# The end of a two-block network on one core: last columns in two quarters, square root on ScalarE, two engines and two queues for the output

## The chip, the cores and the metric

The kernel runs on one core of one Trainium2 chip. The metric is the device time of one execution, in microseconds (us). Three timed runs of the kernel before gave 1130.78, 1130.99 and 1131.72 us; their median, 1130.99 us, is the time before.

## The reference

The program computes two network blocks in fp32 on 256 tokens of width 1024: two hybrid layers (mLSTM, gated linear attention and sparse attention side by side), and then a block of a SwiGLU layer, a mixing layer and a second SwiGLU layer. What the change touches is the very end of it, the down projection of the last SwiGLU layer, its residual sum, and the normalization of the result:

```python
h = h + 0.5 * swiglu(rmsnorm_2(h, ffn2_norm[l]), ffn2_w_gate[l], ffn2_w_up[l], ffn2_w_down[l])
return rmsnorm_2(h, final_norm)

def rmsnorm_2(x, g):
    xf = x.astype(jnp.float32)
    y = xf * lax.rsqrt(jnp.mean(xf * xf, axis=-1, keepdims=True) + EPS)
    return (y * g.astype(jnp.float32)).astype(x.dtype)
```

A row of 1024 numbers can only be scaled once the sum of its squares is known, that is after the last column of the projection has been added to it.

## The kernel before

The 256 tokens are two row tiles of 128 (t = 0, 1), and `x`, the residual stream, stays in SBUF as 128 x 2 x 1024. Every product is made of three fp32r matmuls (`mm3`, L156): weights and activations are split into a high and a low part, and hi x hi, hi x lo and lo x hi are summed in PSUM. Weights come in units of 128 x 1024, which ScalarE copies to the high part (L123) and VectorE reduces to the low part (L124).

`out_proj` makes the last projection. Its output, two tiles by two halves of 512 columns, fills four PSUM banks `op{half}{tile}`. All groups of input rows but the last two run for both tiles at once. The last two groups run bank by bank in the order (t, half) = (0,0), (0,1), (1,0), (1,1), each 12 matmuls of 512 columns (`rows`, two groups of two 128-row slices of three matmuls), so that the banks finish one after the other. After each bank comes `residual` (L333): VectorE reads the 512 columns from PSUM and adds half of them to `x`.

After the second bank of a tile, `write` normalizes the tile through `normed`: ScalarE squares both halves into `xs` (as a throw-away) with a sum per row (L318, an ACTIVATE and the read of its accumulator), VectorE adds the two sums and EPS (L320), GpSimd raises the 128 x 1 result to the power -0.5 (L321), and VectorE scales both halves by it and by the gain (L325, `scalar_tensor_tensor`). Each half goes out through a DMA on SyncE's queue (L1118, 256 KB).

Each engine executes its instructions in the order in which they stand in its program. At this place the order is written out by hand: `out_proj` collects the instructions of ScalarE in a list `act` and those of VectorE in a list `dve`, and `order` chains each list. TensorE's order is that of the calls. The tiles `xs` come from a pool `t2` of 7 slots, `ss` and `r` from the pool `const`. In SBUF the pools lie one behind the other: the weights' (`wr`, `ws`), `big` (with `x` and the transposed activations), `const`, a small gap, `t2`, a gap, and the tiles of the stage (`yh`, `hh`, `fg` and so on).

Of the kernel before, what the change touches and what calls it, by code (L numbers as in the profile page):

```python
# [10 lines left out]
AF = mybir.ActivationFunctionType  # L11
ALU = mybir.AluOpType
# [3 lines left out]
P = 128  # L16
# [4 lines left out]
EPS = 1e-6  # L21
# [3 lines left out]
LEAD = 500  # L25
# [9 lines left out]
class Net:  # L35
# [141 lines left out]
            by_token(t, ps[t])  # L177
        self.tick()

    def rows(self, ps, x, k0, first, last, toks, w):  # L180

        for k in range(2):
            ww = [z[:, 512 * k:512 * (k + 1)] for z in w]
            for t in toks:
                xs = [z[:, k0 + k, P * t:P * (t + 1)] for z in x]
                self.mm3(ps[t], ww, xs, True, first and k == 0, last and k == 1)

    def proj_b(self, x, name, n=2):

# [135 lines left out]
            st.append(nc.vector.scalar_tensor_tensor(xs[h], self.x[:, t, sl], r, g[:, sl], ALU.mult, ALU.mult))  # L325
        return xs, (sq, st, pw)

    def residual(self, t, half, ps, scale=None):
        sl = self.x[:, t, 512 * half:512 * (half + 1)]
        if scale is None:  # L330
            return self.nc.vector.tensor_add(sl, ps, sl)
        else:
            return self.nc.vector.scalar_tensor_tensor(sl, ps, scale, sl, ALU.mult, ALU.add)  # L333

    def out_proj(self, y, nk, scale=None, need=0):


        done = self.begin_next()
        ps = [[self.acc([P, 512], f"op{h}{t}") for t in range(2)] for h in range(2)]
        n = nk // 2  # L340
        for g in range(n - 2):
            if g == need:
                self.join()
            for h in range(2):
                self.rows(ps[h], y, 2 * g, g == 0, False, (0, 1), self.weights())
                self.tick()
        if need >= n - 2:
            self.join()
        ws = [[self.weights() for h in range(2)] for g in range(2)]
        more = self.next_gain is not None  # L350
        units = [self.fetch()] if more else []
        act = [units[0][1][0]] if more else []
        dve = [units[0][1][1]] if more else []
        for t in range(2):
            for h in range(2):
                for g in range(2):
                    self.rows(ps[h], y, 2 * (n - 2 + g), False, g == 1, (t,), ws[g][h])
                    if more and (t, h, g) == (1, 1, 0):
                        units += [self.fetch(), self.fetch(self.third)]
                        act += [units[1][1][0], units[2][1][0]]  # L360
                        dve.append(units[1][1][1])
                        if self.third:
                            self.order([last, units[2][1][1]])
                        for a, b in self.turn():
                            act.append(a)
                            dve.append(b)
                        if not self.third:
                            dve.append(units[2][1][1])
                        dve.append(early)
                with self.tc.high_priority(self.ahead(2 * LEAD)):  # L370
                    early = self.residual(t, h, ps[h][t], scale)
                if not more or (t, h) != (1, 0):
                    dve.append(early)
            if more and t == 1:
                units.append(self.fetch())
                act.append(units[3][1][0])
                dve.append(units[3][1][1])
            self.turn = done(t)
            act += self.steps[0]
            dve += self.steps[1]  # L380
            last = self.steps[2]
        self.order(act)
        self.order(dve)
        self.ready = [u[0] for u in units]
# [722 lines left out]
    def begin_next(self):  # L1107

        if self.next_gain is not None:
            self.xn, fill = self.norm(self.next_gain)  # L1110
            return fill
        g = self.row_bc(self.a["final_norm_2"], D, "g_bc")

        def write(t):
            with self.tc.high_priority(self.ahead(2 * LEAD)):
                halves, self.steps = self.normed(t, g)
                for h, xs in enumerate(halves):
                    self.nc.sync.dma_start(self.out[0, P * t:P * (t + 1), 512 * h:512 * (h + 1)], xs)  # L1118
            return lambda: None

        return write
# [10 lines left out]
def layouts(np, ins):  # L1132
# [18 lines left out]
    for l in range(2):  # L1151
        w = g("w_in")[l]
        m = np.zeros((1024, P), f)
        for o, c, n in ((0, C_IK, 64), (64, C_MLF, 4), (68, C_GA, 16), (84, C_IW, 8), (96, C_MLI, 4)):
            m[:, o:o + n] = w[:, c:c + n]
        misc[64:68, l] = g("ml_b_f")[l]
        misc[96:100, l] = g("ml_b_i")[l]
        units += pa(w, C_DQ) + pb(w, C_IQ, 512) + pb(m, 0, P) + pa(w, C_DK) + pb(w, C_GQ, 256) + pb(w, C_GK, 256)
        head = lambda h: pb(w, C_MLQ + 256 * h, 256) + pb(w, C_MLK + 256 * h, 256)
        units += pa(w, C_DV) + pb(w, C_DZ, 512) + pa(w, C_GV) + pa(w, C_MLV) + pa(w, C_MLO) + head(0) + pa(w, C_GR)  # L1160
        units += pa(w, C_MLV + 512) + head(1) + pa(w, C_MLO + 512) + head(2) + pa(w, C_MLZ) + head(3) + pa(w, C_MLZ + 512)
        units += rows(g("w_out")[l], (1536, 1792, 1024, 1280, 0, 256, 512, 768))

    def ffn(n):
        wg, wu, wd = (g(f"ffn{n}_w_{z}_2")[0] for z in ("gate", "up", "down"))
        out = pa(wg, 0) + pa(wu, 0)
        for c in range(512, DFF, 256):
            out += pb(wg, c, 256) + pb(wu, c, 256)
        return out + rows(wd, range(0, DFF, 256))
# [4 lines left out]
    for n in ("attn", "gmlp"):  # L1174
        wb = g(f"w_branch_{n}_2")[0]
        units += [tiles(wb[:, c:c + 256]) for c in range(0, 1024, 256)]
    units += rows(g("w_out_2")[0], range(0, 1024, 256))
    units += ffn(2)

# [71 lines left out]
```

## Time and profile before

| | |
|---|---|
| median of three runs | 1130.99 us |
| the profiled execution | 1133.35 us |
| its span, first to last instruction | 1131.6 us |
| TensorE busy | 1118.4 us, 99% of the span |
| VectorE busy | 810.8 us, 72% |
| ScalarE busy | 616.3 us, 54% |
| mean granted clock of TensorE | 0.996 of full speed |

The profile is one execution of the program; its times are us from the first instruction. The span is shorter than the execution's time by 1.75 us, which lie before its first and after its last instruction. PE is TensorE, PEld its weight loads, DVE VectorE, ACT ScalarE, POOL GpSimd, SP SyncE, which issues DMAs. Matmuls overlap: each takes longer than the distance to the next. A row of the timeline merges equal instructions that follow each other, and names in brackets what ended the idle time before it.

### The profile page before, as it was taken

The page shows a single profiled execution, that of the slowest core. Times are in us where ns is not written, and L with a number is a line of the kernel's source. Part 1 is how long each engine was busy: PE and PEld are TensorE (multiplying, and loading weights), DVE is VectorE, ACT ScalarE, POOL GpSimd, SP SyncE. Part 2 cuts the span into 40 slices and gives each one's busy share as a digit, 9 for nine tenths or more (in the row PEclk, how much of TensorE's full clock was granted, in tenths as well). Part 3 has the DMA queues.
Part 4 walks back from the last instruction along what each step waited for, and adds up shares of the span by engine and source line. Part 5 has one row for each costly group of instructions (what it writes and reads, how often), then busy time and mean ns, then how long its engine had stood idle before and what let it go on. Part 6 is the DMA issues. An engine that isn't in the chain of part 4 may idle for free.

```text
span 1131.6 us, 16690 instructions
## 1 busy us (share of the span) xinstructions
PE 1118.4 (99%) x6330; PEld 962.3 (85%) x6330; DVE 810.8 (72%) x1233; ACT 616.3 (54%) x950; POOL 105.0 (9%) x136
## 2 busy tenths in 40 slices
PE   8999999999999999999999999999999999999997
PEld 5888889898898989899888888887888998888886
DVE  5688897786568879778747777646698676777743
ACT  4645854564465575456535555444566545555532
POOL 1111102121111210112100000000010001000000
PEclk8999999999999999999999999999999999999999
DMA  8846644455574654455557665666754566666662
GB/s 261 269 151 188 191 153 151 157 168 184 161 216 150 186 182 135 133 160 167 177 165 222 188 191 190 195 188 190 226 182 144 174 189 184 195 188 190 197 190 74
DMA packets 59464, 203.74 MB, mean 180 GB/s; under 512 B 6700, under 2 KB 9652, under 8 KB 59384
## 3 DMA queue, kind: packets, MB, share of 16 engines
q1 hardware_dynamic: 59384, 202.68, 58.3%
q8 instruction: 50, 0.82, 0.3%
q14 instruction: 30, 0.25, 0.1%
HBM read 201.46 MB, written 2.11 MB: 180 GB/s over the span
## 4 chain that ended last, share of the span: by engine, by line
PE 95%; DVE 3%; ACT 1%; DMA 1%; issue 0%; SPq 0%; POOL 0%; DVEq 0%; POOLq 0%; ACTq 0%
PE op L156 20%; PE fg L209 6%; PE fu L209 6%; PE mq L156 4%; PE mk L156 4%; PE mo L156 4%; PE mz L156 4%; PE mv L156 4%; PE fg L210 3%; PE fu L210 3%; PE gatep L209 3%; PE dq L156 2%; PE dz L156 2%; PE brp L156 2%; PE iq L156 2%; PE dk L156 2%
## 5 line engine op out<-in xcount | busy, mean ns | idle before, releaser
L124 DVE TENSOR_TENSOR lo<-raw,hi 128x1024 fp32r<-128x1024 f32 x359 | 443.1, 1236 | 217.1 <-ACT hi L123 216.1
L123 ACT CAST hi<-raw 128x1024 fp32r<-128x1024 f32 x362 | 379.0, 1048 | 371.6 <-PE op L156 91.8
L209 PE MATMUL fu<-x,hi 128*128 128x512 f32 x288 | 101.0, 394 | 0.0
L209 PE MATMUL fg<-x,hi 128*128 128x512 f32 x288 | 100.8, 394 | 0.0
L210 PE MATMUL fg<-x,lo 128*128 128x256 f32 x288 | 79.9, 277 | 0.0
L210 PE MATMUL fu<-x,lo 128*128 128x256 f32 x288 | 79.8, 277 | 0.0
L156 PE MATMUL op<-hi,hh 128*128 128x512 f32 x176 | 68.6, 390 | 0.0
L156 PE MATMUL op<-lo,hh 128*128 128x512 f32 x176 | 68.5, 389 | 0.0
L156 PE MATMUL op<-hi,hl 128*128 128x512 f32 x176 | 68.5, 389 | 0.0
L209 PEld LDWEIGHTS fg<-x,hi 128*128 128x128 f32 x288 | 54.0, 188 | 12.6
L209 PEld LDWEIGHTS fu<-x,hi 128*128 128x128 f32 x288 | 54.0, 188 | 12.5
L321 POOL TENSOR_TENSOR r<-r,mhalf 128x1 f32<-128x1 f32 x12 | 6.7, 555 | 528.5 <-DVE r L320 528.5
L210 PEld LDWEIGHTS fg<-x,lo 128*128 128x128 f32 x288 | 54.1, 188 | 0.1
L210 PEld LDWEIGHTS fu<-x,lo 128*128 128x128 f32 x288 | 54.1, 188 | 0.0
L156 PE MATMUL op<-hi,yh 128*128 128x512 f32 x128 | 51.1, 399 | 0.0
L156 PE MATMUL op<-lo,yh 128*128 128x512 f32 x128 | 50.0, 391 | 0.0
L156 PE MATMUL op<-hi,yl 128*128 128x512 f32 x128 | 49.9, 390 | 0.0
L156 PE MATMUL mq<-x,hi 128*128 128x256 f32 x256 | 48.2, 289 | 0.0
L156 PE MATMUL mk<-x,hi 128*128 128x256 f32 x256 | 46.8, 284 | 0.0
L209 PE MATMUL gatep<-x,hi 128*128 128x512 f32 x128 | 46.1, 403 | 0.0
L697 DVE SCALAR_TENSOR_TENSOR cacc<-pad,cols,cacc 128x256 f32<-128x256 f32 x96 | 41.0, 479 | 0.0
L156 PE MATMUL mv<-hi,x 128*128 128x512 f32 x128 | 40.7, 399 | 0.0
(361 smaller groups left out, 2598.7 us busy)
## 6 DMA issues: line engine op xcount, KB each, us to landing
raw<-in_w SPq DMA_DIRECT2D x362, 512.0 KB, 3.6
x<-in_x SPq DMA_DIRECT2D x2, 512.0 KB, 5.1
g_bc<-in_norm_g SPq DMA_DIRECT2D x2, 512.0 KB, 4.5
mlg<-in_ml_norm_g SPq DMA_DIRECT2D x2, 512.0 KB, 5.1
skew<-strips SPq DMA_DIRECT2D x4, 256.0 KB, 5.2
pen<-skew SPq DMA_DIRECT2D x8, 128.0 KB, 2.9
mb<-M SPq DMA_DIRECT2D x2, 512.0 KB, 4.3
g_bc<-in_ffn_norm SPq DMA_DIRECT2D x2, 512.0 KB
```

Source lines behind the costliest of these rows:

```text
L123: a = nc.scalar.copy(hi, raw)
L124: b = (nc.gpsimd if pool else nc.vector).tensor_tensor(lo, raw, hi.bitcast(F32), ALU.subtract)
L156: self.nc.tensor.matmul(out, lhsT=lhsT, rhs=rhs, start=first and i == 0, stop=last and i == 2)
L209: nc.tensor.matmul(ps, lhsT=wh[:, ks], rhs=self.x2[:, k], start=k == 0, stop=False)
L210: nc.tensor.matmul(ps[:, 1, :], lhsT=wl[:, ks], rhs=self.x2[:, k, 0, :], start=False, stop=k == KT - 1)
L321: pw = nc.gpsimd.tensor_tensor(r, r, self.mhalf[:, 0:1], ALU.pow)
L697: nc.vector.scalar_tensor_tensor(acc[:, c, :], pad[:, c, 1 + i:1 + i + S], w(i), acc[:, c, :], ALU.mult, ALU.add)
```

## The change

The last bank, (t, half) = (1,1), is made in two quarters of 256 columns. The first quarter is finished in its old bank; the last two groups of the second quarter go into a bank of their own, `op_late`, so that the old bank can be read while TensorE writes the new one. The first residual still adds all 512 columns of the old bank (the second quarter has the sum of the earlier groups there), and a second one adds the 256 columns of `op_late`.

The normalization of the last stage is a function of its own, `last`, for both tiles. The sum of squares is taken of three parts, 512, 256 and 256 columns. VectorE multiplies the first half of `x` by the gain before the scale is known (`mult`, L339), and adds EPS and the first two sums (`add`, L340). The third sum goes in as the input and that sum as the bias of a square root on ScalarE (L342); VectorE takes the reciprocal (L343). Then ScalarE scales the first half (L344) and issues its DMA on its own queue (L345), while VectorE scales the second half (L346), which SyncE stores (L347). GpSimd's power falls away here. The lists `act` and `dve` get the new instructions in a written order.

```diff
--- before.py
+++ after.py
@@ -177,13 +177,13 @@
             by_token(t, ps[t])
         self.tick()
 
-    def rows(self, ps, x, k0, first, last, toks, w):
+    def rows(self, ps, x, k0, first, last, toks, w, cols=slice(0, 512)):
 
         for k in range(2):
-            ww = [z[:, 512 * k:512 * (k + 1)] for z in w]
+            ww = [z[:, 512 * k + cols.start:512 * k + cols.stop] for z in w]
             for t in toks:
                 xs = [z[:, k0 + k, P * t:P * (t + 1)] for z in x]
-                self.mm3(ps[t], ww, xs, True, first and k == 0, last and k == 1)
+                self.mm3(ps[t][:, cols], ww, xs, True, first and k == 0, last and k == 1)
 
     def proj_b(self, x, name, n=2):
 
@@ -325,8 +325,32 @@
             st.append(nc.vector.scalar_tensor_tensor(xs[h], self.x[:, t, sl], r, g[:, sl], ALU.mult, ALU.mult))
         return xs, (sq, st, pw)
 
-    def residual(self, t, half, ps, scale=None):
-        sl = self.x[:, t, 512 * half:512 * (half + 1)]
+    def last(self, t, g, out):
+
+
+
+        nc = self.nc
+        x = self.x[:, t, :]
+        ss = self.small([P, 4], "ss4")
+        xs = [self.tmp([P, 512], f"xs{h}") for h in range(2)]
+        hs = [slice(512 * h, 512 * (h + 1)) for h in range(2)]
+        parts = [(0, hs[0]), (1, slice(512, 768)), (1, slice(768, 1024))]
+        sq = [nc.scalar.activation(xs[h][:, c.start - 512 * h:c.stop - 512 * h], x[:, c], AF.Square, scale=1.0 / 32, accum_out=ss[:, i:i + 1]) for i, (h, c) in enumerate(parts)]
+        mult = nc.vector.tensor_tensor(xs[0], x[:, hs[0]], g[:, hs[0]], ALU.mult)
+        add = nc.vector.scalar_tensor_tensor(ss[:, 3:4], ss[:, 0:1], EPS, ss[:, 1:2], ALU.add, ALU.add)
+        r = self.small([P, 2], "r2")
+        root = nc.scalar.activation(r[:, 0:1], ss[:, 2:3], AF.Sqrt, bias=ss[:, 3:4])
+        rec = nc.vector.reciprocal(r[:, 1:2], r[:, 0:1])
+        m = nc.scalar.mul(xs[0], xs[0], r[:, 1:2])
+        nc.scalar.dma_start(out[:, hs[0]], xs[0])
+        st = nc.vector.scalar_tensor_tensor(xs[1], x[:, hs[1]], r[:, 1:2], g[:, hs[1]], ALU.mult, ALU.mult)
+        nc.sync.dma_start(out[:, hs[1]], xs[1])
+        self.marks = mult, add
+        return sq + [root, m], [rec, st], None
+
+    def residual(self, t, half, ps, scale=None, cols=slice(0, 512)):
+        sl = self.x[:, t, 512 * half + cols.start:512 * half + cols.stop]
+        ps = ps[:, cols]
         if scale is None:
             return self.nc.vector.tensor_add(sl, ps, sl)
         else:
@@ -353,6 +377,14 @@
         dve = [units[0][1][1]] if more else []
         for t in range(2):
             for h in range(2):
+                if not more and (t, h) == (1, 1):
+                    late = [None, self.bank([P, 512], "op_late")]
+                    for z, cols in ((ps[h], slice(0, 256)), (late, slice(256, 512))):
+                        for g in range(2):
+                            self.rows(z, y, 2 * (n - 2 + g), z is late and g == 0, g == 1, (t,), ws[g][h], cols)
+                        with self.tc.high_priority(self.ahead(2 * LEAD)):
+                            dve.append(self.residual(t, h, z[t], scale, cols if z is late else slice(0, 512)))
+                    break
                 for g in range(2):
                     self.rows(ps[h], y, 2 * (n - 2 + g), False, g == 1, (t,), ws[g][h])
                     if more and (t, h, g) == (1, 1, 0):
@@ -376,6 +408,10 @@
                 act.append(units[3][1][0])
                 dve.append(units[3][1][1])
             self.turn = done(t)
+            if not more:
+                mult, add = self.marks
+                dve.insert(len(dve) - 2 * t, mult)
+                dve.append(add)
             act += self.steps[0]
             dve += self.steps[1]
             last = self.steps[2]
@@ -1113,9 +1149,7 @@
 
         def write(t):
             with self.tc.high_priority(self.ahead(2 * LEAD)):
-                halves, self.steps = self.normed(t, g)
-                for h, xs in enumerate(halves):
-                    self.nc.sync.dma_start(self.out[0, P * t:P * (t + 1), 512 * h:512 * (h + 1)], xs)
+                self.steps = self.last(t, g, self.out[0, P * t:P * (t + 1)])
             return lambda: None
 
         return write
```

ScalarE's program at its end before; `xs_10683` and `xs_10684` are the halves of tile 0, `xs_10721` and `xs_10722` those of tile 1:

```order
L123 CAST hi<-raw 128x1024 x16
L318 ACTIVATE xs_10683,ss<-x 128x512
L318 ACTIVATE xs_10684,ss<-x 128x512
L318 ACTIVATE xs_10721,ss<-x 128x512
L318 ACTIVATE xs_10722,ss<-x 128x512
```

ScalarE's program at the same place now; tile 1 has `xs_10738` and `xs_10739`:

```order
L123 CAST hi<-raw 128x1024 x16
L338 ACTIVATE xs_10683,ss_10682<-x 128x512
L338 ACTIVATE xs_10684,ss_10682<-x 128x256 x2
L342 ACT_TABLE_LOAD
L342 ACTIVATE r_10690<-ss_10682 128x1
L344 ACTIVATE xs_10683<-xs_10683,r_10690 128x512
L345 DMA out<-xs_10683 128x512
L338 ACTIVATE xs_10738,ss_10737<-x 128x512
L338 ACTIVATE xs_10739,ss_10737<-x 128x256 x2
L342 ACTIVATE r_10745<-ss_10737 128x1
L344 ACTIVATE xs_10738<-xs_10738,r_10745 128x512
L345 DMA out<-xs_10738 128x512
```

Between the squares of tile 0 and those of tile 1 ScalarE now has a table load, the root, a scaling and a DMA; the load stands once, ahead of the first root.

VectorE's program at its end before:

```order
L333 SCALAR_TENSOR_TENSOR x<-op_10304,x 128x512
L333 SCALAR_TENSOR_TENSOR x<-op_10306,x 128x512
L320 SCALAR_TENSOR_TENSOR r<-ss 128x1
L325 SCALAR_TENSOR_TENSOR xs_10683<-x,r,g_bc 128x512
L325 SCALAR_TENSOR_TENSOR xs_10684<-x,r,g_bc 128x512
L333 SCALAR_TENSOR_TENSOR x<-op_10305,x 128x512
L333 SCALAR_TENSOR_TENSOR x<-op_10307,x 128x512
L320 SCALAR_TENSOR_TENSOR r<-ss 128x1
L325 SCALAR_TENSOR_TENSOR xs_10721<-x,r,g_bc 128x512
L325 SCALAR_TENSOR_TENSOR xs_10722<-x,r,g_bc 128x512
```

VectorE's program at the same place now, with the semaphores of engines that each instruction waits for:

```order
L357 SCALAR_TENSOR_TENSOR x<-op_10306,x 128x512 [waits PE_49]
L339 TENSOR_TENSOR xs_10683<-x,g_bc 128x512 [waits Activation_49]
L340 SCALAR_TENSOR_TENSOR ss_10682<-ss_10682 128x1 [waits Activation_49]
L343 RECIPROCAL r_10690<-r_10690 128x1 [waits Activation_49]
L346 SCALAR_TENSOR_TENSOR xs_10684<-x,r_10690,g_bc 128x512 [waits DVE_49]
L357 SCALAR_TENSOR_TENSOR x<-op_10305,x 128x512 [waits PE_49]
L339 TENSOR_TENSOR xs_10738<-x,g_bc 128x512 [waits Activation_49]
L357 SCALAR_TENSOR_TENSOR x<-op_10307,x 128x512 [waits PE_49]
L357 SCALAR_TENSOR_TENSOR x<-op_late,x 128x256 [waits DVE_49,PE_49]
L340 SCALAR_TENSOR_TENSOR ss_10737<-ss_10737 128x1 [waits Activation_49]
L343 RECIPROCAL r_10745<-r_10745 128x1 [waits Activation_49]
L346 SCALAR_TENSOR_TENSOR xs_10739<-x,r_10745,g_bc 128x512 [waits DVE_49]
```

The residual of bank (1,0), `x<-op_10305`, still stands behind tile 0's normalization, now behind its reciprocal and one scaling; the product `xs_10738<-x,g_bc` of tile 1 waits for ScalarE and stands ahead of the residual of the last bank.

On TensorE the last 12 matmuls of 512 columns are now 24 of 256; ahead of them nothing differs in the programs of the engines. In SBUF the new `ss4` and `r2` have two buffers each of 32 bytes (the smallest piece) behind the other tiles of `const`, so the tiles of `t2` and of the stages lie 128 bytes higher (the first slot of `t2` at 111488 in place of 111360).

## Rows read from the trace of the kernel before

**Rows 1.** The page, part 1: each engine's busy time, share, instructions.
```profile
PE 1118.4 (99%) x6330; PEld 962.3 (85%) x6330; DVE 810.8 (72%) x1233; ACT 616.3 (54%) x950; POOL 105.0 (9%) x136
```
**Rows 2.** Timeline, TensorE: start, duration, the last matmuls of banks (1,0) and (1,1).
```profile
1121.40 0.39 PE L156 MATMUL op<-lo,hh 128*128 128x512 f32 x1
...
1124.12 0.39 PE L156 MATMUL op<-lo,hh 128*128 128x512 f32 x1
```
**Rows 3.** Timeline of VectorE from bank (0,1) on.
```profile
1119.10 0.69 DVE L333 SCALAR_TENSOR_TENSOR x<-op,x 128x512 f32<-128x512 f32 x1 [2.03 <-PE op L156]
1120.59 0.16 DVE L320 SCALAR_TENSOR_TENSOR r<-ss 128x1 f32<-128x1 f32 x1 [0.79 <-ACT xs L318]
1121.48 1.41 DVE L325 SCALAR_TENSOR_TENSOR xs<-x,r,g_bc 128x512 f32<-128x512 f32 x2 [0.73 <-POOL r L321]
1122.82 0.68 DVE L333 SCALAR_TENSOR_TENSOR x<-op,x 128x512 f32<-128x512 f32 x1
1124.54 0.69 DVE L333 SCALAR_TENSOR_TENSOR x<-op,x 128x512 f32<-128x512 f32 x1 [1.05 <-PE op L156]
1126.02 0.16 DVE L320 SCALAR_TENSOR_TENSOR r<-ss 128x1 f32<-128x1 f32 x1 [0.79 <-ACT xs L318]
1126.91 1.42 DVE L325 SCALAR_TENSOR_TENSOR xs<-x,r,g_bc 128x512 f32<-128x512 f32 x2 [0.73 <-POOL r L321]
```
**Rows 4.** Timeline of ScalarE: squares of banks (0,1) and (1,1).
```profile
1119.83 0.63 ACT L318 ACTIVATE xs<-x 128x512 f32<-128x512 f32 x1 [2.00 <-DVE x L333]
...
1125.27 0.63 ACT L318 ACTIVATE xs<-x 128x512 f32<-128x512 f32 x1 [1.01 <-DVE x L333]
1125.80 0.19 ACT L318 ACTIVATION_READ_ACCUMULATOR xs<-x 128x1 f32 x1
```
**Rows 5.** Timeline of GpSimd: the power of tile 1.
```profile
1126.33 0.55 POOL L321 TENSOR_TENSOR r<-r,mhalf 128x1 f32<-128x1 f32 x1 [4.88 <-DVE r L320]
```
**Rows 6.** Timeline of SyncE's queue: the last two stores' issues.
```profile
1127.69 0.33 SPq L1118 DMA_DIRECT2D out<-xs  x1
1128.35 0.33 SPq L1118 DMA_DIRECT2D out<-xs  x1
```
**Rows 7.** SyncE's waits from 1115 on: total us, times, longest.
```profile
SPq L1247 <- DMA out<-xs: 1.7, 1, 1.7
```
**Rows 8.** Windows: length, busy (count) by engine, clock, DMA share, GB/s.
```profile
1127.69:1128.52 0.83, 0.00 (x0) 0.00 (x0) 0.64 (x1) 0.00 (x0) 0.00 (x0) 1.00 0.00 0
1128.52:1130.04 1.52, 0.00 (x0) 0.00 (x0) 0.00 (x0) 0.00 (x0) 0.00 (x0) 0.63 0.91 345
```
**Rows 9.** Chain of waits: start, length, piece; 256-column matmuls.
```profile
895.03 23.03 PE brp L156 x192
```
**Rows 10.** Timeline of ScalarE around a table load.
```profile
115.84 1.04 ACT L123 CAST hi<-raw 128x1024 fp32r<-128x1024 f32 x1
116.90 1.28 ACT L640 ACT_TABLE_LOAD   x1
118.19 0.64 ACT L640 ACTIVATE ltmp<-ltmp 128x512 f32<-128x512 f32 x1
```
**Rows 11.** Groups on ScalarE: shapes, count | busy us, mean ns | idle.
```profile
L738 ACT ACTIVATE mjunk<-hp 128x256 f32<-128x256 f32 x16 | 6.5, 407 | 7.4 <-DVE hp L727 7.2
L628 ACT ACTIVATE lg<-lg,smax 128x256 f32<-128x256 f32 x16 | 8.0, 499 | 1.3 <-DVE smax L626 1.3
L519 ACT ACTIVATE iw<-iwT 128x8 f32<-128x8 f32 x4 | 0.5, 168 | 0.0
```
**Rows 12.** Groups on VectorE, the same columns.
```profile
L908 DVE TENSOR_TENSOR fs<-fs,fu 128x512 f32<-128x512 f32 x22 | 15.0, 690 | 0.6
L217 DVE SCALAR_TENSOR_TENSOR qk<-qk2p,qk 128x256 f32<-128x256 f32 x4 | 1.7, 417 | 0.0
```
**Rows 13.** Timeline of VectorE: small instructions that depend on each other.
```profile
550.59 0.16 DVE L724 SCALAR_TENSOR_TENSOR rd<-nd,rd 128x1 f32<-128x1 f32 x1
550.78 0.16 DVE L725 RECIPROCAL rd<-rd 128x1 f32<-128x1 f32 x1
```

## The prediction

> **What bounds the kernel now.** I read the page first: TensorE is busy for 99% of the span [rows 1], so a change behind its last matmul can touch only the last few microseconds. Then the timelines of the engines from 1115 on, as one chain. TensorE starts its last matmul at 1124.12 [rows 2]. VectorE adds the last bank from 1124.54, ScalarE squares it from 1125.27 and has read its sum at 1125.99 [rows 3, 4], VectorE adds the sums at 1126.02, GpSimd's power runs from 1126.33 for 0.55 [rows 5], and VectorE scales both halves from 1126.91 to 1128.33. SyncE issues the two stores at 1127.69 and 1128.35 [rows 6].
>
> What ends last is not the second scaling. From 0.83 after the first issue the 16 DMA engines are 91% busy for 1.52 us, until 1130.04 [rows 8]: the second store's data queue up behind the first's. So the end is set by the first store's issue, plus 0.83, plus 1.52 for 512 KB. SyncE's wait for them is over at 1128.35 + 0.33 + 1.73 = 1130.41 [rows 6, 7], and the barrier behind it ends the span at 1131.6.
>
> The second thing to see is a queue on VectorE: bank (1,0) is complete at about 1121.82 (its last matmul starts 2.72 before that of (1,1), whose residual starts 0.42 after it), but its residual starts at 1122.82 [rows 2, 3], since it stands behind the scalings of tile 0. Before, this lateness dies out: the next residual waits for TensorE again.
>
> **The change, step by step, on the clock of that execution.** Four rules from the rows: an engine starts 0.03 after another's end that released it (1125.23 to 1125.27 in rows 3 and 4); a dependent VectorE instruction 0.03 after the one before it [rows 13]; an independent one about 0.08 before its end (two L325 of 0.75 in 1.41) [rows 3]; the sum of a 512-column square is ready 0.72 after its start [rows 4].
>
> TensorE: 24 matmuls of 256 columns in place of 12 of 512. 192 of 256 took 23.03 [rows 9], so 0.12 each, 2.88 in all against 2.72 for 12: +0.16. A short one is finished a little sooner; `op_late` is complete at about 1124.7 and the old bank at about 1123.25.
>
> Tile 0. The residual of (0,1) ends at 1119.79. Two 256-column squares follow; one takes 0.41 [rows 11], and with their sums they end at about 1120.73. VectorE's product (0.69 [rows 12]) and small sum lie beside them. Then the new thing: Sqrt needs another table, and its load takes 1.28 [rows 10], until 1122.03. The root itself has no row. From below it is the 128x8 ACTIVATE of 0.17, from above the 128x256 one with a bias per row, 0.50 [rows 11]; I take 0.26, the small one plus what such an operand adds (0.499 - 0.407), being nearest to it. Root until 1122.30, reciprocal (0.16 [rows 13]) until 1122.49, scaling of the second half on VectorE from 1122.53 to 1123.28. So bank (1,0)'s residual starts at 1123.20, 0.4 later than now. ScalarE scales its half until about 1123.25 and then issues a DMA; if that holds it as long as SyncE's issue, 0.33 [rows 6], it is free at 1123.6, before it is needed.
>
> Tile 1. Residual (1,0) until 1123.88, its square from 1123.92, its sum at 1124.64. Here is the added wait: the product of `x` and the gain writes the buffer into which the square was thrown away, so VectorE waits for ScalarE, until 1124.67, and then takes 0.69. Behind it stand the residuals of the last bank, of which the first had been ready since 1123.25. It runs from 1125.28 to 1125.97, the second (0.42, the 256-column row [rows 12]) depends on it and runs until 1126.42. TensorE's quarters are ready 2 and 1.3 us before VectorE takes them, so splitting the bank hides nothing as long as VectorE is behind.
>
> The last square starts at 1126.45 and has its sum after 0.49 at 1126.95 (0.41, and 0.08 until its sum is read); the first quarter's square lies before it, the small sum beside it. Root until 1127.24, reciprocal until 1127.43, ScalarE's scaling (0.63 [rows 4] plus 0.09 for the operand per row) until 1128.18 and VectorE's (0.75) until 1128.21. Both stores are issued at about 1128.21 to 1128.24, against 1127.69 and 1128.35 now.
>
> **The two queues.** The pair of stores is bound by 512 KB at 345 GB/s [rows 8] and not by its issues, so issuing them together takes nothing off the 1.52; if anything the earlier first issue of now was worth more. The end moves as the first issue does: 1128.21 - 1127.69 = **+0.52 us**.
>
> The Trainium skill, "DMA: Bandwidth & Descriptors", section "Issuing engines are not separate DMA queues", speaks against this part of the change: DMAs from several issuing engines run on the same 16 DMA engines and only issue time is saved. The trace agrees, with 91% busy. Were the queues separate, the pair would take half of 1.52 and the sum be -0.2.
>
> **Where the time was saved and given back.** From the last residual to the first store the chain gets shorter: now 1124.54 to 1127.69, 3.15; then, from the second quarter's residual at 1126.00 to 1128.21, 2.21. The small residual and square give 0.27 and 0.22, and the sum and the power with their hand-overs (1125.99 to 1126.91, 0.92) become root and reciprocal with theirs (1126.95 to 1127.46, 0.51). That is the 0.9 gained; but the chain starts 1.46 later, at 1126.00 in place of 1124.54. Nearly all of these 1.46 are the table load and the product in front of the residuals.
>
> **Bounds.** With roots of 0.17, +0.34; with roots of 0.50, +1.0. If the scaling costs ScalarE no more than a square, -0.1. If the first DMA on ScalarE's queue needs longer to its data than 0.83, the SyncE store covers it in part. So +0.2 to +1.1. The profiled execution's own time was 1133.35, that is 1131.6 of span and 1.75 around it; it becomes 1133.9 with a span of 1132.1. The median of the runs stands 2.36 lower, and I add the same 0.52: 1131.5.
>
> **Rivals.**
> *The load isn't paid.* If the table is in place before tile 0's squares end, or the load runs beside them, tile 0 is 1.31 earlier, VectorE meets bank (1,0) as it completes, the product is out of the way by 1124.1, and the second quarter is taken at 1124.7: -0.8 us, 1130.2. For it: ScalarE is idle for 2.00 just before the second square of tile 0 [rows 4], room enough for a load. Against: the load stands in its program behind the squares, and it starts only when its turn comes. 12%.
>
> *A switch of tables costs more than the load.* On the path of tile 0 every addition counts in full. In the trace the copy ahead of the load ends at 116.88, the load takes 116.90 to 118.18, and the next one starts at 118.19 [rows 10]: 1.31 in all; against it, then. An addition as large as the load itself would give +0.52 + 1.28, about +1.8: 1132.8. 6%.
> The Trainium skill, "ScalarE: Activation LUTs", section "What ACT_TABLE_LOAD costs", counts 1283 ns and a drain of about 1380 ns, 2.66 us for a switch; by it the sum would be +1.9. The row has the 1283 and no room for the drain.
>
> *The moved tiles cost something.* All tiles behind `const` lie 128 bytes higher, and so does what TensorE reads of them for 1118 us. If each of its 6330 matmuls took 0.4 ns longer, the kernel would be 2.5 us slower, 1133.5; from 0.36 ns on it decides against no change. Against: the products with operands in moved tiles (`brp`, 0.12 each [rows 9]) already run at a steady pace, and nothing in the trace shows that a place costs. 4% for slower by over 0.2%, and as a place may also be better, 3% for faster by as much.
>
> *The change doesn't do what it says:* it does in the order of the programs; that is no case of its own.
>
> **How the numbers follow.** The sum, within its bounds: 75%. No change means within 0.2%, 2.3 us, about what a measurement of this kernel can tell; the sum, the unpaid load and the dearer switch all lie inside it, 93%. Faster by more 3%, slower by more 4%. The likeliest time is 1131.5. The range takes in the unpaid load (1130.2, with 0.3 for the spread of the runs) and the dearer switch (1132.8): 1129.9 to 1132.8.
>
> **What would show it.** In the profile after: an ACT_TABLE_LOAD on ScalarE from about 1120.7 to 1122.0; `x<-op` of bank (1,0) at 1123.2; `xs<-x,g_bc` of tile 1 after a wait for ScalarE at 1124.7; the residual of 512 columns at 1125.3, about 2 us after its last matmul, with no idle time put down to PE; GpSimd idle at the end; two DMA issues, on ScalarE and SyncE, within 0.1 of each other at 1128.2; the DMA engines full for 1.5 us from 1129.0. I am wrong if VectorE waits for TensorE at the last bank, if ScalarE's issue blocks it beyond 1123.9, or if the time differs by more than 2.3 us, which nothing at the end could explain.

## The result

The changed kernel takes 1137.89 us (median of 6 runs, 1136.58 to 1140.92) against 1131.08 before (6 runs, 1130.78 to 1131.72): a ratio of 1.0061 [1.0050, 1.0073], 6.8 us slower. The forecast was 1131.5 within 1129.9 to 1132.8, with 4 chances in 100 for slower. It was wrong. The profiles shown below are of one execution each, 1140.92 us for the changed kernel and 1133.35 for the one before; both lie above their medians.

The end itself went almost as worked out. This is VectorE's timeline of the changed kernel from bank (0,1) on (start, duration, instruction, idle time ahead of it and its releaser), which answers to [rows 3]:

```profile
1125.97 0.69 DVE L357 SCALAR_TENSOR_TENSOR x<-op,x 128x512 f32<-128x512 f32 x1 [2.10 <-PE op L156]
...
1129.25 0.16 DVE L343 RECIPROCAL r<-r 128x1 f32<-128x1 f32 x1 [1.85 <-ACT r L342]
1129.45 0.75 DVE L346 SCALAR_TENSOR_TENSOR xs<-x,r,g_bc 128x512 f32<-128x512 f32 x1
1130.12 0.69 DVE L357 SCALAR_TENSOR_TENSOR x<-op,x 128x512 f32<-128x512 f32 x1
1131.59 0.69 DVE L339 TENSOR_TENSOR xs<-x,g_bc 128x512 f32<-128x512 f32 x1 [0.79 <-ACT xs L338]
1132.20 0.69 DVE L357 SCALAR_TENSOR_TENSOR x<-op,x 128x512 f32<-128x512 f32 x1
1132.99 0.42 DVE L357 SCALAR_TENSOR_TENSOR x<-op_late,x 128x256 f32<-128x256 f32 x1
```

And ScalarE's, its queue included, from the table load to its second store:

```profile
1127.63 1.28 ACT L342 ACT_TABLE_LOAD   x1
1128.92 0.29 ACT L342 ACTIVATE r<-ss 128x1 f32<-128x1 f32 x1
...
1135.26 0.37 ACTq L345 DMA_DIRECT2D out<-xs  x1
```

From the residual of bank (0,1) to the end of the span it was 12.5 us before (1119.10 [rows 3] to 1131.6); now it is 13.1 (1125.97 to 1139.1). The sum said +0.52, the traces say +0.7. What is new starts before that: the same residual comes 6.9 us later. TensorE is the chain up to there, and the chain of waits shows which of its pieces grew. First three pieces of before (start, length, piece, matmuls), all of the output projections `op`, whose matmuls are 128x512 each:

```profile
275.09 28.60 PE op L156 x126
719.36 58.51 PE op L156 x258
1064.64 59.88 PE op L156 x264
```

and the same pieces of the changed kernel, with the 256-column `brp` of [rows 9] between them:

```profile
275.23 29.28 PE op L156 x126
722.87 60.20 PE op L156 x258
899.97 23.04 PE brp L156 x192
1070.17 55.78 PE op L156 x240
```

Length over count: 226.8 to 227.0 ns for a matmul of `op` before, 232.4 to 233.3 now, in every layer, while `brp` stays at 0.12 us. That is 5.4 to 6.6 ns more for each of some 1000 matmuls; summed over all pieces of `op` in the chain, the last compared at 240 matmuls, 5.2 us.

The rest of this execution's loss is in the first feed-forward, in the loop that writes `fg` and `fu`. Groups of TensorE from 622 to 715 us (busy, mean ns of one) have one row of before and one of the changed kernel:

```profile
L209 PE MATMUL fu<-x,hi 128*128 128x512 f32 x132 | 46.3, 394 | 0.0
```
```profile
L209 PE MATMUL fu<-x,hi 128*128 128x512 f32 x128 | 45.7, 399 | 0.0
```

A mean of 399 in place of 394 goes with a pair of matmuls (512 and 256 columns) every 353.3 ns in place of 347.0, which is worked out from the starts in the timeline. Of the 288 pairs of the loop the 264 behind a break differ (the lines are in the last section); that is 1.75 us. Together 5.2, 1.75 and 0.7 make 7.6, against 7.5 between the two profiled spans (1139.1 and 1131.6).

### The profile page after: what moved, and what is told of

Read it like the earlier page. It is cut to its first block, busy times and chain, and to the rows that moved or that the text cites. A ratio compares the mean times of both kernels' runs of the same rounds, so it can differ in the third digit from the quotient of the medians.

```text
span 1139.1 us, 16727 instructions
## 1 busy us (share of the span) xinstructions
PE 1125.6 (99%) x6342; PEld 965.0 (85%) x6342; DVE 811.1 (71%) x1236; ACT 620.4 (54%) x959; POOL 104.0 (9%) x134
## 4 chain that ended last, share of the span: by engine, by line
PE 94%; DVE 3%; ACT 1%; DMA 1%; issue 0%; SPq 0%; POOL 0%; POOLq 0%
PE op L156 20%; PE fg L209 6%; PE fu L209 6%; PE mq L156 4%; PE mk L156 4%; PE mo L156 4%; PE mz L156 4%; PE mv L156 4%; PE fg L210 3%; PE fu L210 3%; PE gatep L209 3%; PE dq L156 2%; PE brp L156 2%; PE dz L156 2%; PE iq L156 2%; PE dk L156 2%
## 5 line engine op out<-in xcount | busy, mean ns | idle before, releaser
L156 PE MATMUL op<-hi,hh 128*128 128x512 f32 (+1 forms) x176 | 69.1, 393 | 0.0
L156 PE MATMUL op<-lo,hh 128*128 128x512 f32 (+1 forms) x176 | 69.0, 392 | 0.0
L156 PE MATMUL op<-hi,hl 128*128 128x512 f32 (+1 forms) x176 | 69.0, 392 | 0.0
L156 PE MATMUL op<-hi,yh 128*128 128x512 f32 x128 | 51.6, 403 | 0.0
L156 PE MATMUL op<-lo,yh 128*128 128x512 f32 x128 | 50.5, 395 | 0.0
L156 PE MATMUL op<-hi,yl 128*128 128x512 f32 x128 | 50.5, 394 | 0.0
L156 PE MATMUL mq<-x,hi 128*128 128x256 f32 x256 | 48.2, 289 | 0.0
L156 PE MATMUL mk<-x,hi 128*128 128x256 f32 x256 | 46.8, 284 | 0.0
L156 PE MATMUL mv<-hi,x 128*128 128x512 f32 x128 | 40.8, 400 | 0.0
L156 PEld LDWEIGHTS mq<-x,hi 128*128 128x128 f32 x256 | 40.2, 191 | 0.4
```

What stands on the lines that cost most here:

```text
L156: self.nc.tensor.matmul(out, lhsT=lhsT, rhs=rhs, start=first and i == 0, stop=last and i == 2)
```

## The experiments

The theory: in the changed kernel, `yh`, `yl`, `hh`, `hl`, `mh` and `ml`, whose slices are the *stationary* operands of `op` (the 128x128 operand that an LDWEIGHTS loads ahead of each matmul; the other one, 512 columns here, is streamed), start 128 bytes off a multiple of 512 bytes of their partition, since `ss4` and `r2` push everything behind `const` up by 128. Before, they lie at multiples of 512, and a 128x128 slice takes 512 bytes of a partition. The rival: the place costs nothing, and the new end or the move as such slows the kernel. The experiments move tiles by the kernel's own unused gaps.

**e1: the changed kernel with the stage tiles back in place**; the slots of `t2` stay 128 bytes off.
```diff
-        self.gap(pool("tail"), 384)
+        self.gap(pool("tail"), 256)
```


> The changed kernel with the gap ahead of the stages' tiles cut from 384 to 256 bytes: the stages' tiles lie where they lay before, the tiles of t2 stay 128 bytes higher, and nothing else differs. Theory A (the projection's matmuls take their stationary operand from y tiles that lie 128 bytes off, and each waits some 6 ns longer): distance of op's matmuls back at 227 ns, time 1131.0 + 0.6 = 1131.7 us. Theory B (the moved t2 tiles): stays at 1136 to 1138. Theory D (something at the end of the kernel): stays at 1136 to 1138.

Measured: 1135.77 (6 runs), 1.0035 [1.0022, 1.0048] to before; `op` back at 227 ns, but the loop of `fg` and `fu` in the first feed-forward again at 353:
```profile
1064.03 54.45 PE op L156 x240
```
The pace of `op` came out as expected, the time did not: it is 4.3 us above before in place of 0.6, so more than the end's share is left.

**e2: the kernel before with the stage tiles alone 128 bytes further on.**
```diff
-        self.gap(pool("tail"), 384)
+        self.gap(pool("tail"), 512)
```


> The kernel before with that gap raised from 384 to 512 bytes: the stages' tiles alone lie 128 bytes higher, the end of the kernel and t2 are as before. Theory A: op's matmuls at 233 ns in place of 227, about 800 of them in the trace's three projections and the last, 1136 to 1137 us. Theories B and D: 1131.

Measured: 1136.79 (4 runs), 1.0049 [1.0034, 1.0064], with not one instruction of the end changed:
```profile
1066.57 61.36 PE op L156 x264
```

**e3: the kernel before with only the y, h and m tiles 128 bytes off**; all other tiles that start at multiples of 512 still do.
```diff
+    def pair(self, n, name):
+        z = self.work([P, 2 * n * S + 128], name, dtype=F32R)
+        return [z[:, 32 + n * S * i:32 + n * S * (i + 1)].rearrange("p (k s) -> p k s", s=S) for i in range(2)]
...
-        yh = self.work([P, 16, S], "yh", dtype=F32R)
-        yl = self.work([P, 16, S], "yl", dtype=F32R)
+        yh, yl = self.pair(16, "yh")
...
```


> The kernel before with the operands of the output projections alone (yh, yl, hh, hl, mh, ml) 128 bytes off, each pair in one tile that is 512 bytes longer; all other tiles keep their place within 512 bytes. Theory A: 1135 to 1137 us, op's matmuls at 233 ns, everything else as before. Theory C (other moved tiles of the stages, which VectorE and ScalarE write, disturb TensorE): 1131.

Measured: 1136.29 (4 runs), 1.0044 [1.0029, 1.0059]. The chain has the slow pieces (the helper's lines shift L156 to L160):
```profile
718.84 59.95 PE op L160 x258
1066.03 61.36 PE op L160 x264
```
61.36 over 264 is 232.4 ns: the place of these tiles alone makes the loss of `op`. It is not the helper that makes it: e10 and e15 below use the same one with the tiles at multiples of 512, and have `op` at 227.

**e4: the kernel before with the stage tiles 512 bytes further on** (384 becomes 896 in the tail gap).

> The kernel before with the gap at 896 bytes: the stages' tiles lie 512 bytes higher, moved but again at multiples of 512. Theory A with a boundary of 512 bytes or less: 1131.0, op's matmuls at 227 ns. If any move costs (a conflict with some other tile's place that was avoided before): 1136 or so.

Measured: 1131.76 (10 runs), 1.0003 [0.9994, 1.0013]:
```profile
1063.43 59.88 PE op L156 x264
```
To the digit the piece of before: moving costs nothing, the place does.

**e8: the kernel before with the stage tiles 256 bytes further on** (384 becomes 640).

> The kernel before with the stage tiles 256 bytes further on, halfway to e4's 512. If the stationary operand has to start at a multiple of 512 bytes: op at 232 to 233 ns, 1136.5 as with 128 bytes. If a multiple of 256 does: op at 227, 1131.4.

Measured: 1133.03 (12 runs) beside 1133.04 of before on that chip, 0.9995 [0.9986, 1.0003]:
```profile
1064.04 59.86 PE op L156 x264
```
A multiple of 256 bytes is enough; 128 is not.

**e5: the kernel before with only the `t2` slots 128 bytes further on.** They were the suspects for the 1.8 us, since the slow loop went with them in the changed kernel and in e1.
```diff
-        self.gap(pool("mid"), 96)
+        self.gap(pool("mid"), 224)
...
-        self.gap(pool("tail"), 384)
+        self.gap(pool("tail"), 256)
```


> The kernel before with only the seven t2 slots 128 bytes further on; the stage tiles stay where they were. Theory T (the place of the t2 slots costs the first feed-forward its 2 us): the pairs of matmuls into fg and fu there at 353.2 ns as in the changed kernel, op at 227, time before + 2.0 us, 1133.4. Rival (the place of t2 costs nothing, and what slows that loop comes with the new end or is chosen in each execution): pairs at 347.4, time as before, 1131.4.

Measured: 1133.32 beside 1133.04, 1.0000 [0.9991, 1.0009]. The profile does show the loop at 353 in the first feed-forward, and in the second too, but the time is that of before. So the timed runs leave no room for a price of 2 us, while the profile shows two slow loops, 3.5 us; the two do not agree, and that stays open. e8, with `t2` untouched, has the second feed-forward at 353, so the slow cadence does not need the move.

**e9 and e11: the changed kernel and the kernel before once more**, unedited, to see whether a kernel has one cadence.

> The changed kernel once more, beside the kernel before on the same chip. Theory (the places of y, h and m in SBUF cost 5.1 us, the new end 0.6, and the loops of fg and fu draw one of two cadences anew in each execution): 5.7 to 7.7 us above before, op at 232 to 233 ns, pairs of fg and fu at 347 or 353 in either feed-forward. Rival (the cadence is fixed by the kernel's layout): as in the changed kernel's first profile, 353.3 in the first feed-forward and 347 in the second.

> The kernel before, one more profile. If a loop's cadence is drawn anew where it starts: the pairs of fg and fu may be at 347 or 353 in either feed-forward, and need not be as in the first profile (347 in both). If the kernel's layout fixes it: 347.4 and 347.3 as in the first profile.

Measured: e9 1139.50 (6 runs), 1.0072 [1.0055, 1.0089]. Its groups from 622 to 715 us and from 968 to 1060:
```profile
L209 PE MATMUL fu<-x,hi 128*128 128x512 f32 x131 | 46.0, 394 | 0.0
...
L209 PE MATMUL fu<-x,hi 128*128 128x512 f32 x128 | 45.7, 399 | 0.0
```
The same kernel, and the slow loop is now in the second feed-forward; in its first profile it was in the first. e11 (one run, 1130.82) has both at 394, as the first profile of before. The kernel alone does not fix which loop is slow. e9's time is 7.4 above before on its chip, within the 5.7 to 7.7 that were expected.

**e12: e5's kernel once more.**

> The kernel of e5 (t2 slots 128 bytes further on), one more profile. If a loop's cadence is drawn anew in each execution: at least one of the loops of ffn1, the mixing layer and ffn2 runs otherwise than in e5. If the layout fixes it: 353.3 in both feed-forwards again.

Measured: 1135.07, both loops at 399 again, what "the layout fixes it" said and not what "drawn anew" said; e9 speaks the other way. A draw, if it is one, is not an even one: of all profiles of this study the eight with `t2` 128 bytes off have at least one slow feed-forward, and of the ten with `t2` in place one has (e8).

**e6 and e13: the changed kernel with `t2` and the stage tiles at their old places of every 512 bytes**, run on two chips. Of the change only the new end is left.
```diff
-        self.gap(pool("mid"), 96)
+        self.gap(pool("mid"), 480)
```


> The changed kernel with 384 bytes more in the gap ahead of t2, so that t2 slots and stage tiles lie 512 bytes further on than before, at the same places of every 512 bytes. Theory (all of the loss but the end's own is layout): op at 227, pairs of fg and fu at 347.4, and only the new end is left, + 0.5 to 0.7 us: 1132.0. Rival (the new end costs more than its rows show, or moves something else): 1134 or more.

> The kernel of e6 again (t2 and stage tiles at their places of before in every 512 bytes, new end). If the new end alone is left: 0.6 above before on this chip, as in e6; loops of fg and fu may be at 347 or 353.

Measured: e6 1133.96 beside 1133.04, 1.0006 [0.9996, 1.0016]; e13 1132.40 beside 1132.84, 0.9998 [0.9987, 1.0009]. With the layout restored the change costs nothing that can be told from zero. From the residual of (0,1) to the end e6 has 13.15 us (1119.35 to 1132.5), the same 0.7 over before as the changed kernel.

**e10 and e15: the changed kernel with only y, h and m back in place**, by e3's helper with an offset of 96 elements.

> The changed kernel with only yh and yl, hh and hl, mh and ml (the stationary operands of op) back at multiples of 512 bytes; the t2 slots and all other stage tiles stay 128 bytes further on. Theory (only the stationary operand's place costs): op at 227, 0.6 us above before, up to 2 more where the loops of fg and fu run the slow cadence. Rival (other moved tiles cost as well): 2 us or more above before in every run.

> The kernel of e10 again (only the stationary operands of op back). As for e14: if only the draw is left, fastest runs at those of e13 within 0.5; if the other moved tiles have a cost of their own, every run 2 or more above, also with the loops at 347.

**e14: e1's kernel once more.**

> The kernel of e1 again (stage tiles back, t2 slots 128 bytes further on, new end). If t2's place sets nothing but the odds of the draw: the fastest runs at the fastest of e13, within 0.5, the median 0 to 3.5 above it. If t2's place has a cost of its own: every run 2 or more above the fastest of e13, also where the profile shows the loops at 347.

Measured: `op` at 227 in all three. e10 1136.07 beside 1132.13, 1.0029 [1.0018, 1.0041]; e15 1134.16 beside 1132.84, 1.0016 [1.0005, 1.0027]; e14 1134.92, 1.0013 [1.0003, 1.0023], where e1, the same program, had 1.0035. The fastest runs of e14 and e15 are 1131.99 and 1132.88, beside 1131.87 of e13. So a fixed price of 2 us for the other moved tiles is excluded: e14's fastest is 0.1 above e13's. e15's is 1.0 above, more than the 0.5 expected, and e10's median is 3.9 above before, more than the 2.6 that the theory allowed it. In the profiles e14 has both loops of `fg` and `fu` at 399, e15 the first, e10 the second, e13 none. The medians above e13 fit slow loops that come more often with `t2` moved, which is argued from these profiles and not shown. One chain of waits, that of e10:
```profile
1064.20 54.42 PE op L160 x240
```

**e7 and e16: the layout restored, the root's table loaded early, and the squares thrown into a tile of their own.** The gap ahead of `t2` is 416 here, since the new small tile takes 64 bytes.
```diff
+        if not more:
+            early_root = self.small([P, 1], "early_root")
+            act.append(self.nc.scalar.activation(early_root, ws[1][1][0][:, 0:1], AF.Sqrt, scale=0.0))
...
-        sq = [nc.scalar.activation(xs[h][:, c.start - 512 * h:c.stop - 512 * h], x[:, c], ...
+        thrown = self.tmp([P, 512], "thrown")
+        sq = [nc.scalar.activation(thrown[:, 0:c.stop - c.start], x[:, c], ...
```


> As e6, and ScalarE takes a square root of zero behind the last weight split, where it idles 5.5 us, and throws the squares into a tile of their own, so that the product of the gain no longer waits for them. If the 1.28 us of the table load and the wait of 0.79 us are what keep the last residuals late: the last residual ends some 1.3 us sooner after the last matmul than in the changed kernel (there 1.84 us), time 1130.7, 0.7 below before. Rival (the two stores' 512 KB set the end whatever the chain): as e6, 1132.0. Rival (the load is paid on ScalarE in another place): 1132.0 or more.

> The kernel of e7 again: 0.7 below before and 1.3 below e13 if its end is what it gained by; as e13 if the stores set the end.

Measured: e7 1132.39 beside 1133.04, 0.9990 [0.9982, 0.9999]; e16 1132.00 beside 1132.84, 0.9992 [0.9983, 1.0000]. That is 0.65 and 0.84 below before, 1.6 below e6 on the one chip and 0.4 below e13 on the other, where 1.3 was expected. ScalarE's timeline of e7 has the load in idle time, and VectorE's has the product without a wait, and at last a residual that waits for TensorE:
```profile
1110.04 1.28 ACT L381 ACT_TABLE_LOAD   x1
...
1120.51 1.23 ACTq L346 DMA_DIRECT2D out<-xs  x1
```
```profile
1121.14 0.69 DVE L340 TENSOR_TENSOR xs<-x,g_bc 128x512 f32<-128x512 f32 x1
1121.75 0.68 DVE L358 SCALAR_TENSOR_TENSOR x<-op,x 128x512 f32<-128x512 f32 x1
1122.94 0.42 DVE L358 SCALAR_TENSOR_TENSOR x<-op_late,x 128x256 f32<-128x256 f32 x1 [0.51 <-PE op_late L156]
```
From the residual of (0,1) it is 11.85 us to the end (1117.35 to 1129.2), 1.3 less than e6: the price of the two steps together, as expected; what each is worth alone was not run. The issue of tile 0's store holds ScalarE 1.23 us here (0.94 in e16, 0.41 in the changed kernel), and the square of bank (1,0) starts behind it; the last residual waits for TensorE, so it is not later for that. It is the fastest version, by little: the intervals reach to 0.9999 and 1.0000.

## Why the prediction was wrong

**The step that failed** is the rival "The moved tiles cost something", and the sentence "nothing in the trace shows that a place costs". The sum has no term for the place of the tiles. The move was seen, its price (0.4 ns on all 6330 matmuls, 2.5 us) was chosen by hand, and the chance was 4%. The evidence against it was `brp` [rows 9]. But `brp` reads the moved tiles as the streamed operand, and its pace of 0.12 is indeed the same after. The matmuls that suffer are those of `op`, whose *stationary* operand moved, and in the kernel before that operand lies at multiples of 512 bytes alone. So the row could not speak against the rival; the price had no bound from above, and the range should have reached to it. What the runs showed in its place: not 0.4 ns on all matmuls, but 5.6 ns in the long pieces of `op` (232.4 ns in e3 beside 226.8 in e4 and e8); over the 1008 matmuls of `op` that is some 5 us, 5.2 in the changed kernel's chain. The prediction's last sign of being wrong, more than 2.3 us that nothing at the end explains, is what came.

**"Ahead of them nothing differs in the programs"** was true of the instructions and misled me: they are the same, their addresses are not, and TensorE is the bound for 99% of the span [rows 1]. There each ns on a thousand matmuls is 1 us, as much as the whole end is about.

**The end: the mechanism was right, the size nearly.**
- The table load is paid in tile 0, 1.28 as in [rows 10], with 1.29 from its start to the root's: no dearer switch. That rival falls, and "the load isn't paid" with it; e7 shows that this one was a matter of the program, not of the chip.
- The root takes 0.29; I took 0.26 between 0.17 and 0.50.
- Residual (1,0) was to be 0.4 late through tile 0's chain. Its distance from that of (0,1) is 4.15 (1125.97 to 1130.12), 0.43 more than in [rows 3].
- The product waits 0.79 for ScalarE and stands ahead of both last residuals, neither of which waits for TensorE: as predicted.
- ScalarE's DMA issue holds it 0.41 instead of 0.33, before it is needed.
- The last residual starts 0.10 behind its predecessor's end in place of 0.03, and each root takes 0.03 more; such small overruns add up to the 0.2 between +0.52 and +0.7.

**The stores.** Both are issued within 0.1 of each other, and then the engines move them as before; the windows of the changed kernel (length, busy by engine, clock, DMA share, GB/s) answer to [rows 8]:
```profile
1135.26:1136.20 0.94, 0.00 (x0) 0.00 (x0) 0.01 (x1) 0.00 (x0) 0.00 (x0) 0.72 0.05 20
1136.20:1137.70 1.50, 0.00 (x0) 0.00 (x0) 0.00 (x0) 0.00 (x0) 0.00 (x0) 0.50 0.87 337
```
and SyncE's last wait, which answers to [rows 7]:
```profile
SPq L1281 <- DMA out<-xs: 2.3, 1, 2.3
```
337 GB/s for two queues, 345 for one. From the first issue to the end of the wait it is 2.7 in both. The two queues move no more than one, as the trace of before had it. The Trainium skill ("DMA: Bandwidth & Descriptors", "Issuing engines are not separate DMA queues") has it that DMAs of several issuing engines run on the same 16 DMA engines, and the 337 beside 345 GB/s agree with it. No run here has the new end with one queue.

**What stays open:** how a loop comes by one of the two cadences told below, and why the place of `t2` should favour the slow one (8 of 8 profiles against 1 of 10). TensorE does read a moved tile of `t2` in these loops: the eight transposes `hT`, behind which the cadence can change, take `fs` from it as their stationary operand. The eight take 1.03 us in both kernels, so their own pace is the same; whether their operand's place sets what follows was not tested. Nor do the timed runs add up: `t2` moved alone costs nothing (e5), the new end alone next to nothing (e6, e13), and both together, with `op` at 227 ns, have medians 2.1 and 4.3 us above before (e14 and e1), and 1.3 and 3.9 where the other stage tiles are moved as well (e15 and e10). Slow loops are the likely rest of the changed kernel's 6.8 us beside 5.2 and 0.7; that is argued from profiles, not isolated.

## What to carry to other kernels

A new small tile moves all that is allocated behind it. In a kernel bound by TensorE, look where its stationary operands start in SBUF before and after every change of allocation, and put new tiles behind them or pad to 256 bytes. This is shown for the 512-column fp32r matmuls of `op` alone: the transposes `hT`, whose operand moved too, did not slow down. Evidence that an operation is indifferent to something counts only for the same operand in the same role. At an end that is a chain over several engines, first take out what stands ahead of the last piece (here a table load and a borrowed buffer, 1.3 us together), since splitting that piece pays nothing until then.

## What the hardware showed unexpectedly

**A loop of matmuls has two cadences, and a break can change the one for the other.** The loop of `gatep`, which alternates 512 and 256 columns with a new stationary operand each time, shows both in one execution of the kernel before. TensorE's timeline, the 512-column matmuls alone:
```profile
847.66 0.40 PE L209 MATMUL gatep<-x,hi 128*128 128x512 f32 x1
...
848.36 0.40 PE L209 MATMUL gatep<-x,hi 128*128 128x512 f32 x1
...
849.05 0.40 PE L209 MATMUL gatep<-x,hi 128*128 128x512 f32 x1
...
852.04 0.40 PE L209 MATMUL gatep<-x,hi 128*128 128x512 f32 x1
...
853.10 0.40 PE L209 MATMUL gatep<-x,hi 128*128 128x512 f32 x1
...
856.99 0.40 PE L209 MATMUL gatep<-x,hi 128*128 128x512 f32 x1
```
Four pairs from 847.66 to 849.05 take 347 ns each, then other work comes between, and fourteen from 852.04 to 856.99 take 354. The fast one repeats every two pairs (350 and 343 ns), the slow one every three (350, 361 and 349).

The feed-forwards show the same. In all 36 of them (two in each of the eighteen profiles) the first 24 pairs of the loop are slow; then eight transposes `hT` come between, and the cadence behind them holds for the other 264 pairs. TensorE's timeline in the first feed-forward, of the kernel before and below it of the changed one: the first and the last 512-column matmul ahead of the break, the break, and two matmuls 23 pairs apart behind it.
```profile
618.33 0.39 PE L209 MATMUL fg<-x,hi 128*128 128x512 f32 x1
...
626.44 0.40 PE L209 MATMUL fu<-x,hi 128*128 128x512 f32 x1
...
626.81 1.03 PE L232 MATMUL hT<-ident,fs 128*128 128x128 f32 x8
...
628.02 0.40 PE L209 MATMUL fu<-x,hi 128*128 128x512 f32 x1
...
636.00 0.39 PE L209 MATMUL fu<-x,hi 128*128 128x512 f32 x1
```
```profile
620.09 0.39 PE L209 MATMUL fg<-x,hi 128*128 128x512 f32 x1
...
628.20 0.40 PE L209 MATMUL fu<-x,hi 128*128 128x512 f32 x1
...
628.56 1.03 PE L232 MATMUL hT<-ident,fs 128*128 128x128 f32 x8
...
629.78 0.40 PE L209 MATMUL fu<-x,hi 128*128 128x512 f32 x1
...
637.91 0.40 PE L209 MATMUL fu<-x,hi 128*128 128x512 f32 x1
```
Ahead of the break 23 pairs take 8.11 us in both kernels; behind it they take 7.98 and 8.13. Behind the break twelve of the 36 are slow, 93.00 us in place of 91.25 from the first pair to the last. They stand in nine of the eighteen profiles: both of the changed kernel, e1, e5, e8, e10, e12, e14 and e15.

**An early stretch at half clock comes and goes.** The kernel before in its first profile, and below it the same stretch of e9:
```profile
12.80:19.50 6.70, 6.13 (x15) 4.35 (x14) 5.30 (x9) 2.86 (x4) 0.69 (x1) 0.50 0.88 237
```
```profile
12.80:19.50 6.70, 5.57 (x25) 4.32 (x25) 5.33 (x9) 2.48 (x3) 0.75 (x1) 1.00 0.90 236
```
At 0.50 (1.2 GHz) TensorE starts 15 matmuls here, at 1.00 (2.4 GHz) 25; ahead of both it works with pauses. The kernel before took 1133.35 with the stretch and 1130.82 without (e11), both loops fast in each. This and the cadence are likely to be much of why single runs of one kernel lie up to 5.9 us apart (1130.88 to 1136.75 for before beside e13). A dozen runs beside 35 of before leave about 1 us of doubt either way here (e13: 0.9987 to 1.0009), so a difference under 1 us needs more.
